# A bidirectional RWKV-7 step: the next block's keys, decays and rates issued from inside the scan

## The chip, the cores and the metric

The program runs on one core of a Trainium2 chip. Its time is device time in microseconds, from launch to end of one execution. A profile is one execution taken by the hardware profiler; its span goes from the first to the last instruction, and what lies around it (some 2 us here) counts in the time but not in the span.

The engines are TensorE (PE in the profile, with its weight loads as PEld), VectorE (DVE), ScalarE (ACT), GpSimd (POOL) and SyncE (SP, which issues most of the transfers). Each works through its own queue in order, and semaphores tie the queues together.

## The reference

One layer of a diffusion backbone for 128 context tokens and 256 latent tokens with D_MODEL = 2048. A modulated RMS norm gives h; one wide projection `h @ w_in` gives the inputs of two branches; a short gated convolution (B) and an RWKV-7 mixer (A) are projected, merged by sigmoid gates and projected once more. The part that the change touches is branch A:

```python
w_lin = w0 + einsum('btdr,drc->dbtc', tanh(wd), w2)
decay = exp(-exp(-softplus(-w_lin) - 0.5))          # = exp(-e^-0.5 * sigmoid(w_lin))
a     = sigmoid(a0 + einsum('btdr,drc->dbtc', ad, a2))
kk    = k * k_k;  kk = kk / max(|kk| per head, 1e-12)
k_dir = k * (1 + (a - 1) * k_a)
# per direction, head and token:
S = S * decay + (S @ -kk) (kk * a)^T + v k_dir^T ;  y = S @ r
```

The recurrence runs forward and backward over the tokens, for 32 heads of 64 channels. Context starts from a zero state, latent tokens from a cached one. The two directions are summed, normalised per head, a bonus term is added, and the result is gated.

## The kernel before

**Layout.** Channels lie on the 128 partitions, the 384 tokens (context, then latent) along the free dimension. Branch A goes in 16 blocks of 128 channels (two heads each). Tokens go in six chunks of 64 (NCH = 6, C = 64): two of context and four latent ones. The scan is in chunk form: within a chunk the recurrence becomes triangular matrices that are inverted, between chunks a 64 x 64 state per head is carried.

**Dense stream.** `Stream` is a generator of groups of three matmuls (`mm3`, lines 81 to 83: high part by high, low by high, high by low; 128 x 384 each). It works through the wide projections, two column tiles of 128 at a time: `rk` (r and k of a block), `gv` (gate and v), and the fills `bc`, `bx`, `bg`, `gb`, `ma`, `mb` and later `ob`, `oa`. Weights are loaded by SP into two `raw` buffers and split by `split` into a high part (a cast on ACT, line 88) and a low part (a subtraction on DVE, line 89), with three buffers of each. `ds_.go(n)` emits n groups; these cover the waits of the scans.

**A block.** For block b the main loop (lines 938 to 961) runs:

- `prep_b(b)`: products of keys, rates and decays into `bk` and `pr` (lines 667 to 674), the chunk matrices `pA` (695), masked into `A` (701), and the inversion of their 32 x 32 diagonal pieces on DVE (716, 718) by way of DRAM.
- `prep_c(b)`: transposes and the value products.
- `prep_a(b + 1)`, as soon as `gv` of block b is done: for the next block the squares of the keys, the low-rank products for decay and rate and their sigmoids (`sig`, 628), the per-head norm by a matmul (`pn`, 633 and 634), floored on DVE (`kn`, 636). Its tail is elementwise: three reciprocals (638), a product with the keys (639), and for each direction a cumulative sum over a chunk (646), two exponentials on ACT (`ep`, 648; `em`, 649, written over `sig`), the direction's key `kd` (651, 652) and the rate product (653).
- `scan(b)`: the off-diagonal corners of the inverses and then the chunk chains.
- `norm(b)`; `finish(b)` follows inside the next block.

**The scan.** First the matmuls `pH` (line 847, recorded at 843) and four copies into `x11` (849), alternately on ACT and DVE; three groups of the dense stream (H0 = 3); the first state product `po` of the latent chain (805) with its sum on DVE (806); three more groups; the bonus sum `pbn` (856, 857) with `bon` on DVE (859); the matmuls `pX` (861, recorded at 843) and four copies into the corners of `A` (863), again alternately on ACT and DVE: the first two fill the corners of the even blocks of A, the others those of the odd ones. Four groups follow (H1 = 4), and then the two chains, context and latent, take turns. A step of a chain is one of: `po` (805) followed by a sum on DVE (806); `pq` (822) with A, followed by copies on ACT (824); `pu` (829) followed by a new state on DVE (832 or 834). Two groups of the dense stream lie behind each step while both chains run, four when one is left. `ls` (810) scales the old state on ACT.

**What sets the order.** PE's order is the order in which the program emits its instructions (`manual_schedule` for PE). For all other engines and for the transfers that they issue, a planner makes the order ahead of time: it takes, among the instructions that it reckons ready, the one with the best priority, which is the place in the program; `tc.high_priority(offset=300)`, which `drive(scan(b, cur), 300)` puts around the scan's own instructions, moves those 300 places forward. The order so found is fixed in the queues, whatever the real durations are. `tc.issue_after(ins)` adds for each instruction in its scope that runs on the engine of `ins` the rule that it stands behind `ins` in that queue.

Of the kernel before, what the change touches and what calls it, by code (L numbers as in the profile page):

```python
# [20 lines left out]
NB = 16  # L21
C = 64
# [34 lines left out]
def hybrid_step(ctx, tc, cst, x_prompt, x_sample, state_f, state_b, c, c_ctx, ada_w, ada_b, norm_g,  # L57
# [3 lines left out]
    V, S, G, TE = nc.vector, nc.scalar, nc.gpsimd, nc.tensor  # L61
# [339 lines left out]
    r_, k_, v_, ga_ = {}, {}, {}, {}  # L401
# [206 lines left out]
    def prep_a(b, o):  # L608

        bs = slice(b * P, (b + 1) * P)  # L610
        r, k, v = r_[b], k_[b], v_[b]
        kk = sp.tile([P, T], F32, tag="kk", name=f"kk_{b}")
        S.mul(kk[:], k[:], pcol(KK + b))
        sq = tmp(f"sq_{b}")
        S.activation(sq[:], kk[:], AF.Square)
        sqh, sql = hl_parts(sq, sp.tile([P, T], F32R, tag="hl", name=f"sqh_{b}"), f"sq_{b}")
        sig = []
        for m in range(4):
            if m % 2 == 0:
                lraw = sp.tile([96, 2, P], F32, tag="lraw", name=f"lraw_{b}_{m}")  # L620
                nc.sync.dma_start(lraw[:], (w2, a2)[m // 2][0][:, :, bs].rearrange("d r n -> r d n"))
                lwh, lwl = split(lraw[:], [96, 2, P], "lwh", "lwl", sp, f"{b}_{m}", rows=96)
                yield 2
            pl = bank(f"pl_{b}_{m}")
            pl = flat(pl[:, 0:3, :])
            mm3(pl, lwh[:, m % 2, :], lwl[:, m % 2, :], l_hi[:, m, :], l_lo[:, m, :], True, True)
            t = tmp(f"sig_{b}_{m}")
            S.activation(t[:], pl, AF.Sigmoid, bias=pcol((W0, W0 + 16, A0, A0 + 16)[m] + b))
            sig.append(t)
            yield 2  # L630
        pn = bank(f"pn_{b}")
        pn = flat(pn[:, 0:3, :])
        TE.matmul(pn, bones_r[:], sqh[:], start=True, stop=False)
        TE.matmul(pn, bones_r[:], sql[:], start=False, stop=True)
        kn = sp.tile([P, T], F32, tag="kn", name=f"kn_{b}")
        V.tensor_scalar(kn[:], pn, 1e-24, None, ALU.max)
        for q in range(3):
            V.reciprocal(kn[:, q * P:(q + 1) * P], kn[:, q * P:(q + 1) * P])
        V.scalar_tensor_tensor(kn[:], kk[:], -1.0, kn[:], ALU.mult, ALU.mult)
        o.update(kk=kk, ep=[], em=[], kd=[], bn=[])  # L640
        for d in range(2):
            def nat(a):
                return a[:, ::-1] if d else a[:]
            sg, aa = sig[d], sig[2 + d]
            L = tmp(f"L_{b}_{d}")
            V.tensor_tensor_scan(L[:], segm, sg[:], 0.0, op0=ALU.mult, op1=ALU.add)
            ep = eps_[b % 2, d]
            S.activation(ep[:, :, 1:C + 1], c3(L[:]), AF.Exp, scale=-DECAY)
            S.activation(sg[:], L[:], AF.Exp, scale=DECAY)
            kd = tmp(f"kd_{b}_{d}")  # L650
            V.tensor_scalar(kd[:], aa[:], pcol(KA + b), omka[:, b:b + 1], ALU.mult, ALU.add)
            V.tensor_tensor(kd[:], nat(k), kd[:], ALU.mult)
            V.tensor_tensor(aa[:], nat(kn), aa[:], ALU.mult)
            o["ep"].append(ep)
            o["em"].append(sg)
            o["kd"].append(kd)
            o["bn"].append(aa)
# [127 lines left out]
    def scan(b, o):  # L785
# [72 lines left out]
        bon = sp.tile([P, T], F32, tag="bon", name=f"bon_{b}")  # L858
        V.tensor_tensor(bon[:], pbn, v_[b][:], ALU.mult)
        o["bon"] = bon  # L860
        pz = corner("pX", lambda f, h: x11[32:64, 2 * f + h, :], lambda f, h: A[32:64, 0, f, C * h + 32:C * h + C])
        for j in range(4):
            (S.copy, V.tensor_copy)[j % 2](A[0:32, 0, j // 2::2, C * (j % 2) + 32:C * (j % 2) + C], pz[j])
        yield H1

        live = [chain(0), lat]
# [54 lines left out]
        V.tensor_tensor(ya[:], ya[:], ga_[b][:], ALU.mult)  # L921
        nc.sync.dma_start(ya_d[b], ya[:])

    def drive(gen, prio=0):
        n = 0
        while True:
            with tc.high_priority(offset=prio):
                u = next(gen, None)
            if u is None:
                return n  # L930
            ds_.go(u)
            n += u

    ds_.go(PRO)
    cur = {}
    drive(prep_a(0, cur))
    prev = None
    for b in range(NB):
        if b < NB - 1:
            if b > 0:  # L940
                ds_.urgent += [(add_rk, b + 1), (add_gv, b)]
        if b == NB - 2:
            ds_.fills += [(add_gv, NB - 1)] + [(add_ob, g) for g in range(8)]
        pb_gen = prep_b(b, cur)
        ds_.go(next(pb_gen))
        if prev is not None:
            finish(b - 1, prev)
        drive(pb_gen)
        n = drive(prep_c(b, cur))
        nxt = {}  # L950
        if b < NB - 1:
            while f"gv{b}" not in ds_.done:
                ds_.go(1)
                n += 1
            n += drive(prep_a(b + 1, nxt))
        w = WINDOW + (FIRST if b == 0 else LAST if b == NB - 1 else 0)
        if n < w:
            ds_.go(w - n)
        drive(scan(b, cur), 300)
        norm(b, cur)  # L960
        prev, cur = cur, nxt
    ds_.go(12)
# [180 lines left out]
```

## Time and profile before

| | us |
|---|---|
| three runs | 2264.18, 2262.54, 2259.86 |
| their median | 2262.54 |
| profiled execution, time | 2259.46 |
| profiled execution, span | 2257.7 |
| PE busy (matmuls) | 2187.7 (97%) |
| PE busy (weight loads) | 2072.2 (92%) |
| DVE busy | 1522.4 (67%) |
| ACT busy | 1048.9 (46%) |
| POOL busy | 118.6 (5%) |

The mean granted clock of PE was 0.996. The profile gives, for each line of the kernel, engine and operation, how often it ran, its busy time, the mean length of one in ns, and the engine's idle time just ahead of it with the work that ended it. A wait is written as `engine tile line <- releaser: us in total, times, longest us`. A row of a timeline is `start, length, engine, line, operation, output <- inputs, count`, with the idle time ahead in brackets.

### The profile page before, as it was taken

The numbers are of one execution on the slowest core, as the hardware profiler recorded it, in microseconds if no ns is written. First come the engines' busy times: TensorE is split into PE (matmuls) and PEld (weight loads), VectorE is DVE, ScalarE is ACT, GpSimd is POOL, SyncE is SP. The second block draws the span as 40 slices with busy tenths as digits, with TensorE's granted clock in tenths as the row PEclk, the third lists the DMA queues.
The fourth block names the chain that finished last, engine by engine and source line by source line (L and its number), as shares of the span: only waits on it lengthen the run. The fifth ranks groups of instructions, "written<-read, shape, count | busy, mean of one in ns | idle before, by whom it ended". The sixth has DMA issues, their size and how long they took to land.

```text
span 2257.7 us, 40435 instructions
## 1 busy us (share of the span) xinstructions
PE 2187.7 (97%) x16084; PEld 2072.2 (92%) x16084; DVE 1522.4 (67%) x3096; ACT 1048.9 (46%) x1852; POOL 118.6 (5%) x115
## 2 busy tenths in 40 slices
PE   5999999999999999999999999999999999999998
PEld 3588999999999999999999999999999899889988
DVE  3249567777777778776878687777767774444444
ACT  4246445454545455454545454545455543333233
POOL 2001010101010100000010101010100000000000
PEclk9999999999999999999999999999999999999999
DMA  9963544444444444353444444444445465985633
GB/s 334 347 203 116 147 137 126 114 121 114 110 132 112 125 116 126 105 132 102 122 108 132 111 112 127 113 115 141 121 118 143 133 187 161 309 299 190 219 131 113
DMA packets 429646, 339.97 MB, mean 151 GB/s; under 512 B 84801, under 2 KB 411025, under 8 KB 428561
## 3 DMA queue, kind: packets, MB, share of 16 engines
q1 hardware_dynamic: 427968, 335.62, 50.6%
q8 instruction: 127, 2.08, 0.4%
q10 hardware_dynamic: 432, 1.57, 0.2%
q14 instruction: 63, 0.51, 0.1%
q0 software_dynamic: 1056, 0.19, 0.1%
HBM read 307.37 MB, written 29.36 MB: 149 GB/s over the span
## 4 chain that ended last, share of the span: by engine, by line
PE 90%; DMA 5%; DVE 2%; issue 2%; SPq 1%; ACT 1%; POOLq 0%; POOL 0%; DVEq 0%; ACTq 0%
PE d_rk L81 4%; PE d_gv L81 4%; PE d_gv L83 4%; PE d_gv L82 4%; PE d_rk L83 4%; PE d_rk L82 4%; DMA raw_adah<-in_ada_w_dram 3%; PE d_oa L81 2%; PE d_bx L81 2%; PE d_bg L81 2%; PE d_bc L81 2%; PE d_mb L81 2%; PE pq L822 2%; PE d_bg L83 2%; PE d_bg L82 2%; PE d_bx L83 2%
## 5 line engine op out<-in xcount | busy, mean ns | idle before, releaser
L716 DVE TENSOR_TENSOR ut<-U 48x30 f32<-48x30 f32 (+14 forms) x480 | 154.6, 322 | 16.2 <-DMA U<-ui 4.2
L81 PE MATMUL d_rk<-h_hi,whi_rk 128*128 128x384 f32 x480 | 164.3, 342 | 0.6 <-ACT lst L549 0.6
L718 DVE TENSOR_TENSOR U<-U,ut 48x30 f32<-48x30 f32 (+14 forms) x480 | 154.3, 321 | 10.8
L81 PE MATMUL d_gv<-h_hi,whi_gv 128*128 128x384 f32 x480 | 161.1, 336 | 0.0
L83 PE MATMUL d_gv<-h_hi,wlo_gv 128*128 128x384 f32 x480 | 160.8, 335 | 0.0
L82 PE MATMUL d_gv<-h_lo,whi_gv 128*128 128x384 f32 x480 | 160.7, 335 | 0.0
L83 PE MATMUL d_rk<-h_hi,wlo_rk 128*128 128x384 f32 x480 | 160.5, 334 | 0.0
L82 PE MATMUL d_rk<-h_lo,whi_rk 128*128 128x384 f32 x480 | 160.5, 334 | 0.0
L88 ACT CAST whi_gv<-raw_gv 128x1024 fp32r<-128x1024 f32 (+1 forms) x64 | 64.0, 999 | 141.1 <-PE d_rk L82 93.9
L89 DVE TENSOR_TENSOR wlo_rk<-raw_rk,whi_rk 128x1024 fp32r<-128x1024 f32 x60 | 72.9, 1218 | 44.6 <-ACT whi_rk L88 35.5
L88 ACT CAST whi_rk<-raw_rk 128x1024 fp32r<-128x1024 f32 x60 | 63.0, 1053 | 78.7 <-PE d_bx L82 16.4
L910 POOL TENSOR_TENSOR rs<-var,nhalf 128x6 f32<-128x6 f32 x16 | 21.2, 1326 | 1370.2 <-DVE var L908 1370.2
L81 PE MATMUL d_bg<-h_hi,whi_bg 128*128 128x384 f32 x256 | 92.8, 363 | 0.0
L81 PE MATMUL d_gb<-h_hi,whi_gb 128*128 128x384 f32 x256 | 92.5, 361 | 0.0
L81 PE MATMUL d_bc<-h_hi,whi_bc 128*128 128x384 f32 x256 | 92.4, 361 | 0.0
L81 PE MATMUL d_bx<-h_hi,whi_bx 128*128 128x384 f32 x256 | 92.3, 361 | 0.0
L81 PE MATMUL d_ma<-h_hi,whi_ma 128*128 128x384 f32 x256 | 92.0, 359 | 0.0
L81 PEld LDWEIGHTS d_rk<-h_hi,whi_rk 128*128 128x128 f32 x480 | 90.1, 188 | 1.8 <-ACT lst L549 0.9
L81 PEld LDWEIGHTS d_gv<-h_hi,whi_gv 128*128 128x128 f32 x480 | 90.5, 189 | 0.2
L81 PE MATMUL d_mb<-h_hi,whi_mb 128*128 128x384 f32 x256 | 90.6, 354 | 0.0
L82 PEld LDWEIGHTS d_gv<-h_lo,whi_gv 128*128 128x128 f32 x480 | 90.4, 188 | 0.0
L83 PEld LDWEIGHTS d_gv<-h_hi,wlo_gv 128*128 128x128 f32 x480 | 90.4, 188 | 0.0
(320 smaller groups left out, 6649.5 us busy)
## 6 DMA issues: line engine op xcount, KB each, us to landing
raw_adah<-in_ada_w_dram SPq DMA_DIRECT2D x64, 512.0 KB, 8.7
raw_rk<-in_w_in_dram SPq DMA_DIRECT2D x60, 512.0 KB, 5.3
raw_gv<-in_w_in_dram SPq DMA_DIRECT2D x60, 512.0 KB, 5.0
raw_ma<-in_w_in_dram SPq DMA_DIRECT2D x16, 1024.0 KB, 5.5
raw_mb<-in_w_in_dram SPq DMA_DIRECT2D x16, 1024.0 KB, 5.4
raw_bc<-in_w_in_dram SPq DMA_DIRECT2D x16, 1024.0 KB, 5.6
raw_bx<-in_w_in_dram SPq DMA_DIRECT2D x16, 1024.0 KB, 5.5
raw_bg<-in_w_in_dram SPq DMA_DIRECT2D x16, 1024.0 KB, 5.4
```

Source lines behind the costliest of these rows:

```text
L81: TE.matmul(out, wh, xh, start=start, stop=False)
L82: TE.matmul(out, wh, xl, start=False, stop=False)
L83: TE.matmul(out, wl, xh, start=False, stop=stop)
L88: S.copy(hi[0:rows], src)
L89: V.tensor_tensor(lo[0:rows], src, hi[0:rows].bitcast(F32), ALU.subtract)
L716: V.tensor_tensor(tv, U[:, 0:s, s:s + 1].broadcast_to([48, s, w]), U[:, s:s + 1, s + 1:].broadcast_to([48, s, w]), ALU.mult)
L718: V.tensor_tensor(U[:, 0:s, s + 1:], U[:, 0:s, s + 1:], tv, ALU.add)
L822: TE.matmul(pq[:, d, :], A[:, 0, f, :], sav[:, f, :], start=True, stop=True)
L910: G.tensor_tensor(rs[:], var[:], nhalf[:], ALU.pow)
```

## The change

`prep_a` is cut in two behind the floor on the norm (line 636). What stood behind it (lines 637 to 657: reciprocals, product with the keys, cumulative sums, exponentials, keys and rate products) becomes `prep_k`. For block 0 it is called right behind `prep_a`. For blocks 1 to 15 it is called from inside the scan of the block before: `drive` gets a step (3) and a function, and calls it ahead of the scan's fourth step, when the scan has emitted the four copies of line 863 and the four groups behind them. There `prep_k` is emitted at ordinary priority, with the rule that its ACT instructions stand behind the last ACT copy and its DVE instructions behind the last DVE copy. No instruction is added to or taken from the computation.

```diff
     def prep_a(b, o):
 ...
         kn = sp.tile([P, T], F32, tag="kn", name=f"kn_{b}")
         V.tensor_scalar(kn[:], pn, 1e-24, None, ALU.max)
+        o.update(kk=kk, kn=kn, sig=sig)
+
+    def prep_k(b, o):
+
+        k, kk, kn, sig = k_[b], o["kk"], o["kn"], o["sig"]
         for q in range(3):
             V.reciprocal(kn[:, q * P:(q + 1) * P], kn[:, q * P:(q + 1) * P])
         V.scalar_tensor_tensor(kn[:], kk[:], -1.0, kn[:], ALU.mult, ALU.mult)
-        o.update(kk=kk, ep=[], em=[], kd=[], bn=[])
+        o.update(ep=[], em=[], kd=[], bn=[])
         for d in range(2):
 ...
+        o["turn"] = [None, None]
         pz = corner("pX", lambda f, h: x11[32:64, 2 * f + h, :], lambda f, h: A[32:64, 0, f, C * h + 32:C * h + C])
         for j in range(4):
-            (S.copy, V.tensor_copy)[j % 2](A[0:32, 0, j // 2::2, C * (j % 2) + 32:C * (j % 2) + C], pz[j])
+            o["turn"][j % 2] = (S.copy, V.tensor_copy)[j % 2](
+                A[0:32, 0, j // 2::2, C * (j % 2) + 32:C * (j % 2) + C], pz[j]).ins
         yield H1
 ...
-    def drive(gen, prio=0):
-        n = 0
+    def drive(gen, prio=0, at=None, fn=None):
+        n = i = 0
         while True:
+            if i == at:
+                fn()
+            i += 1
             with tc.high_priority(offset=prio):
                 u = next(gen, None)
 ...
     drive(prep_a(0, cur))
+    prep_k(0, cur)
 ...
-        drive(scan(b, cur), 300)
+
+        def keys():
+
+            with tc.issue_after(cur["turn"][0]), tc.issue_after(cur["turn"][1]):
+                prep_k(b + 1, nxt)
+
+        drive(scan(b, cur), 300, 3 if b < NB - 1 else None, keys)
```

More of the change, by code (lines that the diff above doesn't have):

```diff
@@ L610, in prep_a @@
         bs = slice(b * P, (b + 1) * P)
-        r, k, v = r_[b], k_[b], v_[b]
+        k = k_[b]
         kk = sp.tile([P, T], F32, tag="kk", name=f"kk_{b}")
```

## The prediction

> **What bounds the kernel now.** I read the page's shares and chain first, then the waits of PE and of its weight loads, then the timelines of two blocks, one that waits at the corners and one that does not.
>
> ```profile
> span 2257.7 us, 40435 instructions
> PE 2187.7 (97%) x16084; PEld 2072.2 (92%) x16084; DVE 1522.4 (67%) x3096; ACT 1048.9 (46%) x1852; POOL 118.6 (5%) x115
> PE 90%; DMA 5%; DVE 2%; issue 2%; SPq 1%; ACT 1%; POOLq 0%; POOL 0%; DVEq 0%; ACTq 0%
> ```
>
> PE carries 90% of the chain that ended last. The change adds no matmul, takes none away and moves none (prep_k holds none), so PE's order stays as written and only its waits can change. Of PE's 2257.7 - 2187.7 = 70.0 us without a matmul, this window of the loop over the blocks (its length, then busy PE) holds 1707.0 - 1685.1 = 21.9:
>
> ```profile
> 203.00:1910.00 1707.00, 1685.08 (x13166) 1645.32 (x13167) 1273.66 (x2701) 849.92 (x1548) 87.63 (x61) 1.00 0.45 125
> ```
>
> There one wait stands out; first the waits of the weight loads, then those of the matmuls:
>
> ```profile
> PEld pq L822 <- issue: 19.5, 10, 2.3
> PEld pX L843 <- issue: 3.7, 11, 1.2
> ...
> PE pq L822 <- issue: 16.6, 10, 2.0
> ```
>
> The first pq of the scan waits in 10 of 16 blocks. "issue" says that the profile found no releaser, so I look for it in the timeline of one such block (the third): PE, then DVE, then ACT.
>
> ```profile
> 479.70 0.82 PE L843 MATMUL pX<-A,x 32*32 32x32 f32 x48
> 484.80 0.68 PE L822 MATMUL pq<-sav,A 128*128 128x128 f32 x4 [1.97 <-issue]
> ...
> 475.97 2.57 DVE L638 RECIPROCAL kn<-kn 128x128 f32<-128x128 f32 x3
> ...
> 481.33 0.94 DVE L646 TENSOR_TENSOR_SCAN L<-cs,sig 128x384 f32<-128x384 f32 x1
> 482.19 0.52 DVE L667 TENSOR_TENSOR bk<-sig,sig 128x384 f32<-128x384 f32 x1
> 482.64 1.21 DVE L89 TENSOR_TENSOR wlo_gb<-raw_gb,whi_gb 128x1024 fp32r<-128x1024 f32 x1
> 483.78 0.54 DVE L859 TENSOR_TENSOR bon<-pbn,v 128x384 f32<-128x384 f32 x1
> 484.35 0.35 DVE L863 COPY A<-pX 32x192 f32<-32x192 f32 x1
> ...
> 482.36 0.53 ACT L648 ACTIVATE ep<-L 128x384 f32<-128x384 f32 x1 [0.39 <-DVE L L646]
> 482.79 0.51 ACT L649 ACTIVATE sig<-L 128x384 f32<-128x384 f32 x1
> 483.20 0.39 ACT L88 CAST lwh<-lraw 96x256 fp32r<-96x256 f32 x1
> 483.62 0.31 ACT L863 COPY A<-pX 32x192 f32<-32x192 f32 x1
> ```
>
> pX has ended at 480.52. Its first corner copy (ACT) starts only at 483.62, because ACT stands in its queue at the exponentials of L648, which wait for the scan L646, and that stands on DVE behind the reciprocals. The second copy (DVE, 484.35) ends at 484.70, and pq, which for its first chunk needs the even blocks of A, that is these two copies, starts 0.10 us later. So the corner copies release PE, and what is ahead of them is the next block's prep.
>
> **What the wait costs.** Now a block (the fifth) that does not wait, PE and then DVE:
>
> ```profile
> 694.96 0.62 PE L843 MATMUL pX<-A,x 32*32 32x32 f32 x48
> 697.70 0.60 PE L822 MATMUL pq<-sav,A 128*128 128x128 f32 x4
> ...
> 700.69 0.61 PE L829 MATMUL pu<-sav,bt 128*128 128x128 f32 x4
> ...
> 703.68 0.61 PE L805 MATMUL po<-st,pr 128*128 128x128 f32 x4
> ...
> 706.66 0.60 PE L822 MATMUL pq<-sav,A 128*128 128x128 f32 x4
> ...
> 696.87 0.35 DVE L863 COPY A<-pX 32x192 f32<-32x192 f32 x1
> ...
> 702.56 0.59 DVE L832 COPY st<-pu 64x128 f32<-64x128 f32 x2
> ...
> 705.93 0.42 DVE L806 TENSOR_TENSOR sav<-po,sav 64x256 f32<-64x256 f32 x1
> ```
>
> From pX to pq it takes 2.74 us, in the waiting block 5.10: 2.36 more, where the weight loads' longest wait is 2.3. I therefore take the weight loads' sum, 19.5 us. In one block the wait fell inside pX instead: 1.2 us, the longest of that row; its other ten (2.5 us together) are hand-overs that stay. I add 1.0.
>
> The clock adds one term. These are two windows of the third block: the stretch, its length, busy time of PE, PEld, DVE, ACT and POOL with their instructions, the granted clock, the DMA share and GB/s:
>
> ```profile
> 484.00:492.00 8.00, 7.20 (x38) 7.23 (x39) 7.15 (x16) 3.10 (x8) 0.00 (x0) 0.79 0.17 32
> 492.00:520.00 28.00, 28.00 (x217) 27.64 (x216) 17.42 (x35) 12.37 (x26) 0.00 (x0) 1.00 0.39 116
> ```
>
> Right behind this one wait PE ran at 0.79 over 8 us: 8 x 0.21 = 1.7 us. [...]
>
> Gain if all of it goes: 19.5 + 1.0 + 1.7 = 22.2 us.
>
> **The change part by part.** For 15 of 16 blocks the tail of prep_a is issued behind the second pair of corner copies. Its instructions:
>
> ```profile
> L638 DVE RECIPROCAL kn<-kn 128x128 f32<-128x128 f32 x48 | 43.6, 932 | 0.5
> L639 DVE SCALAR_TENSOR_TENSOR kn<-kk,kn 128x384 f32<-128x384 f32 x16 | 8.9, 554 | 0.3
> L646 DVE TENSOR_TENSOR_SCAN L<-cs,sig 128x384 f32<-128x384 f32 x32 | 30.2, 945 | 0.0
> L651 DVE TENSOR_SCALAR kd<-sig,par,omka 128x384 f32<-128x384 f32 x32 | 14.9, 465 | 0.0
> L652 DVE TENSOR_TENSOR kd<-k,kd 128x384 f32<-128x384 f32 x32 | 17.1, 535 | 0.1
> L653 DVE TENSOR_TENSOR sig<-kn,sig 128x384 f32<-128x384 f32 x32 | 17.4, 545 | 0.1
> ...
> L648 ACT ACTIVATE ep<-L 128x384 f32<-128x384 f32 x32 | 16.8, 525 | 14.3 <-DVE L L646 14.1
> L648 ACT ACT_TABLE_LOAD x16 | 20.5, 1283 | 5.4 <-DVE L L646 5.3
> L649 ACT ACTIVATE sig<-L 128x384 f32<-128x384 f32 x32 | 16.4, 513 | 0.1
> L863 ACT COPY A<-pX 32x192 f32<-32x192 f32 x32 | 9.9, 310 | 17.4 <-DVE A L863 12.4 <-PE pX L843 4.7
> ```
>
> The last row is a copy that stays. Per block, by busy time over 16: DVE (43.6 + 8.9 + 30.2 + 14.9 + 17.1 + 17.4) / 16 = 8.3 us in 12 instructions; ACT (16.8 + 20.5 + 16.4) / 16 = 3.4 us. No DMA is issued by it, and nothing on POOL or in SP's queue moves past it.
>
> *Ahead of the copies* this goes away. DVE keeps the maximum on kn, copies, bon and the splits. With the queues clear, the four copies follow pX one after another, as each waits for the one before (12.4 us of ACT's idle time is put down to DVE's copy): about 0.35 us each (0.31 on ACT, 0.35 on DVE), and the second ends near 0.9 us after pX's end, 1.5 after its start. pq is due 2.74 after it. The margin is 1.2 us, which is one split (1.21) that may still stand in the way. I cost new waits at pq at nothing; without that margin they would be a few tenths.
>
> *Behind the copies* 8.3 us of DVE work now stand among the first steps of the two chains. In the fifth block a step's result has from po (703.68) to pq (706.66), 2.98 us; less 0.61 for the matmuls and 0.42 for the sum of L806, some 1.95 us are free. There L806 began at 705.93, that is 1.64 us after po's end at 704.29, and PE did not wait: 0.3 us were left. Before the change that late start came from a DVE queue that had been full since ahead of the corner; now it begins clear at the copies, and the full stretch begins there. The scan's own instructions stand 300 higher in priority, so among ready ones they go first, but a queue written ahead of time can be late by as much as the real durations exceed those it was planned by. No row of the changed order exists, so I bound it: at best nothing (steps stay inside 1.95 us); at worst all 8.3 us stand ahead of the first L832. Copies end 2.1 after pX, the burst at 10.4, L832 (0.6) at 11.0; po is due at 703.68 - 694.96 = 8.7 after pX: 2.3 us a block, 15 blocks, 34 us. I take 0.2 us a block, 3 us, much nearer the low end, because in the fifth block much the same DVE work, with the chains' instructions in it, made this step 1.64 late and cost nothing.
>
> *ACT*: table load and exponentials wait for L646, some 4 us behind the copies, then hold ACT for up to 3.4. The copies L824 of both chains are due before (pq at 2.74 and about 1.5 later), the next at 706.66 - 694.96 = 11.7. If that cover goes, the price is one step of up to 1.3.
>
> *Late next*: the next block's bk products (L667, L668) move from about 482 to about 495; their reader, the next pA, is at 525. DVE is busy 17.4 of the 28 us from 492 to 520, so 10.6 are free for some 7 shifted. The split L89 comes later too, with two of three weight buffers filled ahead. Both cost nothing; without that room pA would wait for the excess, up to a few us.
>
> Sum: 22.2 - 3 = 19.2. The profiled execution took 2259.46 us (span 2257.7), so 2240.3 for one like it; the median of the runs shown is 3.1 higher, at 2262.54, and gives **2243.3**.
>
> **The rivals.**
> (a) *Half taken back*: the chains' steps wait about 0.9 us a block; 22.2 - 15 x 0.9 = 9 us, 2254. For it speaks the 0.3 us left in the fifth block; against it the many later steps that start at once.
> (b) *No change*: another full queue takes the place of the prep. If DVE's splits and ACT's casts, ready at that time, are issued into the gap, two of them (1.21 + 1.05) ahead of the copies spend the margin and another microsecond; with what the chains lose the gain is 22.2 - 10 x 1.1 - 15 x 0.5 = 4, 2259 or above. Or the order does not do what it says because the copies were late for another cause; the 0.10 us between copy and pq speak against that.
> (c) *Slower*: the moved burst holds the first chain steps. The place is L832 and L806 behind the reciprocals; price 34 us at worst, 2262.5 - 22.2 + 34 = 2274; it decides once the wait passes 22.2 / 15 = 1.5 us a block, since all 15 blocks pay and only ten gain. Against it: prep_k's instructions are short ones (0.95 at most) between which the planner can put the chains'. [...]
>
> **How the numbers follow.** Forecast 0.62; (a) 0.15; (b) 0.12; (c) 0.11. A measurement of this kernel can tell about 0.2%, 4.5 us, from no change, so faster means below 2258: forecast and (a), 0.77; within 0.12; slower 0.11. The range runs from 2238 (22.2 us gained, nothing lost, and some 2 us for the runs' scatter of 2259.86 to 2264.18) up to 2257, where (a) ends: 2238 to 2257, leaving out most of (b) and (c), 0.2.
>
> **What would show it.** Right: the pq row of L822 among the waits falls from 19.5 to under 3; the second copy of L863 stands within 1.5 us of pX's start; pX to pq is 2.74 in all blocks; the reciprocals stand behind the copies; no granted clock below 1 behind a corner. Small waits of po, pq or pu by DVE L832, L834 or L806 of 0.2 us a block would fit. Wrong: such waits above 1.5 us a block (c), or corner copies still 3 us behind pX with splits or casts ahead of them (b); pA waiting for L667 would mean that the shifted work found no room.

## The result and the profile after

| | before | after |
|---|---|---|
| median of the runs of the comparison, us | 2264.05 (2259.86 to 2268.76) | 2250.85 (2248.88 to 2255.54) |
| ratio to before, 95% interval | 1 | 0.9941 [0.9925, 0.9957] |
| profiled execution, time, us | 2259.46 | 2250.97 |
| profiled execution, span, us | 2257.7 | 2249.2 |

The changed kernel is faster by 13.2 us by the medians (9.7 to 17.0 by the interval), against 19.2 forecast. 2250.85 lies in the range and 7.6 above the predicted 2243.3. Of the runs further down, prio and sig each had one execution of more than double the time (6369.04 and 5683.89 us), which the medians count and the ratios leave out.

The head of the page of the changed kernel and the chain that ended last:

```profile
span 2249.2 us, 40427 instructions
PE 2191.4 (97%) x16084; PEld 2071.0 (92%) x16084; DVE 1522.2 (68%) x3096; ACT 1060.7 (47%) x1864; POOL 115.5 (5%) x115
PE 84%; DVE 6%; DMA 6%; ACT 2%; issue 1%; SPq 1%; POOLq 0%; POOL 0%; DVEq 0%; ACTq 0%
```

PE carries 84% of the chain instead of 90%, DVE 6% instead of 2%. A kernel that had only lost its waits would show more of PE. The 12 further instructions on ACT are table loads, 45 of 1283 ns each where before has 33; in the trace of after they stand at the exponentials of L653 (22 of them) and at the sigmoids of lines 258, 434, 480 and 488 (23). The waits of PE's weight loads in the loop say where DVE and ACT came in:

```profile
PEld pu L834 <- ACT sav L829: 8.2, 11, 0.9
PEld pA L700 <- issue: 6.3, 30, 0.2
...
PEld pq L827 <- DVE sav L811: 3.8, 6, 0.8
...
PEld po L810 <- issue: 3.0, 7, 0.6
```

(Lines have moved by 5 to 7: 822 is now 827, 829 is 834, 805 is 810, 863 is 869, 646 is 651, 832 is 837, 882 is 889.) The row of 19.5 us, pq behind the corner copies, is gone. In its place are three rows that did not stand there before: pu waiting for the copies of pq on ACT, pq for the sum of po on DVE, and po, where the row names no releaser; in the eighth block po waits for the new state on DVE (L839), at 1028.95. They are steps of the chains, behind the corner.

The eighth block is one where this is seen whole. PE, then DVE, then ACT:

```profile
1008.15 0.62 PE L848 MATMUL pX<-A,x 32*32 32x32 f32 x48
1010.97 0.68 PE L827 MATMUL pq<-sav,A 128*128 128x128 f32 x4
...
1020.66 0.71 PE L827 MATMUL pq<-sav,A 128*128 128x128 f32 x4 [0.45 <-DVE sav L811]
...
1024.33 0.71 PE L834 MATMUL pu<-sav,bt 128*128 128x128 f32 x4 [0.41 <-ACT sav L829]
...
1041.86 1.62 PE L889 MATMUL py<-sav,A 128*64 128x64 f32 x48
```

```profile
1010.52 0.35 DVE L869 COPY A<-pX 32x192 f32<-32x192 f32 x1 [1.05 <-ACT A L869]
...
1011.53 2.55 DVE L643 RECIPROCAL kn<-kn 128x128 f32<-128x128 f32 x3
1014.01 0.88 DVE L651 TENSOR_TENSOR_SCAN L<-cs,sig 128x384 f32<-128x384 f32 x1
1014.82 1.19 DVE L89 TENSOR_TENSOR wlo_bg<-raw_bg,whi_bg 128x1024 fp32r<-128x1024 f32 x1
1016.04 0.59 DVE L837 COPY st<-pu 64x128 f32<-64x128 f32 x2
...
1019.21 0.95 DVE L651 TENSOR_TENSOR_SCAN L<-cs,sig 128x384 f32<-128x384 f32 x1
1020.19 0.42 DVE L811 TENSOR_TENSOR sav<-po,sav 64x256 f32<-64x256 f32 x1
```

```profile
1009.75 0.41 ACT L88 CAST lwh<-lraw 96x256 fp32r<-96x256 f32 x1 [1.57 <-DMA lraw<-in_w_dram]
1010.18 0.31 ACT L869 COPY A<-pX 32x192 f32<-32x192 f32 x1
...
1014.19 1.28 ACT L653 ACT_TABLE_LOAD   x1
1015.49 0.52 ACT L653 ACTIVATE ep<-L 128x384 f32<-128x384 f32 x1
...
1020.19 0.52 ACT L653 ACTIVATE ep<-L 128x384 f32<-128x384 f32 x1 [1.24 <-DVE L L651]
1020.74 0.53 ACT L822 COPY ytok<-po 64x128 f32<-64x128 f32 x2
1021.18 0.52 ACT L654 ACTIVATE sig<-L 128x384 f32<-128x384 f32 x1
1021.61 1.04 ACT L88 CAST whi_bg<-raw_bg 128x1024 fp32r<-128x1024 f32 x1
...
1023.11 0.62 ACT L464 ACTIVATE bu<-bc,par 128x384 f32<-128x384 f32 x1
1023.75 0.53 ACT L829 COPY sav<-pq 64x128 f32<-64x128 f32 x2
```

The corner is as forecast: both first copies are done at 1010.87, pq starts at 1010.97, 2.82 after pX, and the reciprocals stand behind the copies. The cost comes later, on two queues:

- **DVE**: reciprocals, one scan and a split stand ahead of the first state copy (L837, at 1016.04). The second scan ends only at 1020.16, and right behind it the sum L811, at 1020.19, is already late for pq.
- **ACT**: the second direction's exponentials wait 1.24 us for that scan and stand, with copies to ytok and a cast between them, and an instruction of the convolution branch (L464) behind them, ahead of the copy L829. pq had ended at 1020.66 + 0.71 = 1021.37, and its copy starts at 1023.75, 2.4 us later. pu waits for it. The exponentials themselves fill only the first 0.3 of these 2.4 us; the rest is other work that stands ahead of the copy in the queue and was held up with it.

**A measure for the rest of the text.** An undisturbed block takes 33.1 us from the start of pX to the end of its last py: in the fifth block of before, where pX starts at 694.96, py stands at

```profile
726.46 1.62 PE L882 MATMUL py<-sav,A 128*64 128x64 f32 x48
```

so 726.46 + 1.62 - 694.96 = 33.1. In the eighth block above it is 1041.86 + 1.62 - 1008.15 = 35.3, an excess of 2.2. Summed over the 16 blocks, the excess is 23.0 in before and 14.7 in after; at the corner (pX to pq beyond 2.74) it is 20.1 and 0.1. The rest of the loop takes the same in both (1090.1 and 1090.6). Of before's 23.0, 20.1 lie at the corner, 1.7 in the clock behind the third block's corner wait, and 1.2 in small waits of 0.1 to 0.2 a block. The first two are gone; the small ones have grown from 1.2 to 14.6. So 13.4 us came back in the chains, 0.9 us a block in 15 blocks.

### The profile page after: what moved, and what is told of

It reads as the page before. It is cut to its first block, busy times and chain, and to the rows that moved or that the text cites. A ratio compares the mean times of both kernels' runs of the same rounds, so it can differ in the third digit from the quotient of the medians.

```text
span 2249.2 us, 40427 instructions
## 1 busy us (share of the span) xinstructions
PE 2191.4 (97%) x16084; PEld 2071.0 (92%) x16084; DVE 1522.2 (68%) x3096; ACT 1060.7 (47%) x1864; POOL 115.5 (5%) x115
## 3 DMA queue, kind: packets, MB, share of 16 engines
q8 instruction: 127, 2.08, 0.4%
## 4 chain that ended last, share of the span: by engine, by line
PE 84%; DVE 6%; DMA 6%; ACT 2%; issue 1%; SPq 1%; POOLq 0%; POOL 0%; DVEq 0%; ACTq 0%
PE d_rk L81 4%; PE d_rk L83 4%; PE d_rk L82 4%; DMA raw_adah<-in_ada_w_dram 4%; PE d_gv L81 4%; PE d_gv L83 4%; PE d_gv L82 4%; PE d_oa L81 2%; PE pA L700 2%; PE d_oa L83 2%; PE d_oa L82 2%; PE d_mb L81 2%; PE d_bc L81 2%; PE d_gb L81 2%; PE d_bg L81 2%; PE d_mb L83 2%
```

## The experiments

Every kernel below has its profiled time, the excess as defined (summed over its 16 blocks by its own trace), its waits of the weight loads of po, pq and pu together (each from 0.1 us up, so that a sum can be some tenths above the rows shown), and the median and ratio of its runs. "Time less excess" is what the kernel would take without the waits, and the falls of the clock, inside the scans.

| kernel | profiled time | excess | time less excess | waits of po, pq, pu | median | ratio to before |
|---|---|---|---|---|---|---|
| before | 2259.46 | 23.0 | 2236.5 | 19.6 | 2264.05 | 1 |
| again | 2266.31 | 26.5 | 2239.8 | 21.1 | one run | - |
| after | 2250.97 | 14.7 | 2236.3 | 15.5 | 2250.85 | 0.9941 [0.9925, 0.9957] |
| after2 | 2251.18 | 13.0 | 2238.2 | 13.9 | 2253.41 | 0.9952 [0.9940, 0.9964] |
| prio | 2257.70 | 18.2 | 2239.5 | 15.4 | 2257.49 | 0.9974 [0.9965, 0.9984] |
| sig | 2250.12 | 11.9 | 2238.2 | 12.9 | 2252.32 | 0.9950 [0.9937, 0.9964] |
| recip | 2250.26 | 12.7 | 2237.6 | 13.6 | 2252.66 | 0.9951 [0.9938, 0.9963] |
| marks | 2254.19 | 14.4 | 2239.8 | 14.0 | 2255.10 | 0.9963 [0.9949, 0.9977] |
| both | 2247.54 | 9.4 | 2238.1 | 9.5 | 2249.37 | 0.9937 [0.9925, 0.9949] |
| late | 2244.02 | 4.0 | 2240.0 | 3.7 | 2244.57 | 0.9916 [0.9902, 0.9929] |
| split | 2240.78 | 1.1 | 2239.7 | 0.5 | 2241.42 | 0.9903 [0.9889, 0.9916] |

The fourth column stays within 2236.3 to 2240.0 while the excess goes from 26.5 to 1.1: in these kernels the time follows the excess, about 1 us for 1 us. (h1, cover and half change PE's order itself and stand further down.)

### The kernel before once more (again)

No edit; one profile of the unchanged kernel.

> The kernel before, unchanged, for a second profile. Open: the profiled executions differ by 8.5 us in span (2257.7 and 2249.2), the medians by 13.2. Theory (clock): a corner wait of about 2 us sometimes drops PE's clock for some us; the first profile has this behind one of ten waits (granted clock 0.79 over 8 us, 1.7 us lost), another execution has it behind more, and its span is longer by some 1.7 us for each: with 2264 us, two to four drops. Rival: no more than one drop, and the span is longer elsewhere (the loading prologue, the tail).

The excess is 26.5, 3.5 more than in the first profile, with the same corner part (19.9). What differs is the clock. The three longest corner waits (2.4 us from pX to pq beyond 2.74) fall in blocks 3, 7 and 11; behind all three PE runs slower here, where the first profile shows it behind the first of them alone. The windows behind those three waits in the second profile, and then behind the first two of them in the first (stretch, length, busy PE, PEld, DVE, ACT, POOL, granted clock, DMA share, GB/s):

```profile
484.00:489.00 5.00, 4.69 (x21) 4.72 (x22) 4.97 (x10) 2.40 (x6) 0.00 (x0) 0.66 0.00 0
911.00:916.00 5.00, 5.00 (x26) 5.00 (x25) 4.31 (x9) 2.09 (x5) 0.00 (x0) 0.66 0.01 2
1338.00:1343.00 5.00, 5.00 (x25) 5.00 (x24) 4.26 (x10) 1.88 (x5) 0.00 (x0) 0.66 0.08 7
```

```profile
484.00:489.00 5.00, 4.20 (x20) 4.23 (x21) 4.94 (x11) 2.40 (x6) 0.00 (x0) 0.73 0.00 0
911.00:916.00 5.00, 4.76 (x32) 4.79 (x33) 4.94 (x11) 2.41 (x6) 0.00 (x0) 1.00 0.01 2
```

Each costs 5 x 0.34 = 1.7 us. So the change removes, beside the waits, one to three of these drops, and which of them an execution has is not the same from one to the next (what decides it was not shown). That is part of why the medians differ by 13.2 us where the two profiles differ by 8.5. The time less excess also differs, by 3.3, between the two profiles of the same kernel; that lies outside the scans of the loop's blocks and isn't the change's. One such part is a fall of the clock behind a wait of pv ahead of the last block's scan: again has it (at 1819, the wait 2.5 us), the profile of after too (0.50 from 1806.45 to 1809.87, the wait 2.9 us), the first profile of before has not (the wait 2.4 us).

### Only the place in the program (prio)

`prep_k` called where the change calls it, without the rule on the queues:

```diff
-            with tc.issue_after(cur["turn"][0]), tc.issue_after(cur["turn"][1]):
-                prep_k(b + 1, nxt)
+            prep_k(b + 1, nxt)
```

> prep_k emitted at the scan's fourth step as in the change, but without the two rules that put it behind the corner copies. Theory (the rule does it): the planner takes prep_k's instructions as soon as they are ready, ahead of the copies, and the wait of the first pq is back at 15 to 20 us by the weight loads; ratio to before 0.998 to 1.002. Rival (the place in the program does it): the copies go first by priority alone, the wait stays at 0, ratio 0.994 as in the change.

14.7 of the 20.1 us stay at the corner, a little less than expected, and the ratio is a little below the 0.998 expected. In the third block the planner takes the reciprocals and the first scan into DVE's idle time ahead of the copies all the same:

```profile
476.09 2.57 DVE L643 RECIPROCAL kn<-kn 128x128 f32<-128x128 f32 x3
...
481.45 0.94 DVE L651 TENSOR_TENSOR_SCAN L<-cs,sig 128x384 f32<-128x384 f32 x1
...
484.48 0.35 DVE L869 COPY A<-pX 32x192 f32<-32x192 f32 x1
```

So it is the rule on the queues that moves the work. The later place alone gives 0.9974, about half of the change's gain.

### No table loads, and fewer reciprocals behind the corner (sig, recip)

Two candidates for what the chains wait for. In sig the exponentials of the moved part become sigmoids, so that they need no table load in these blocks; the decays then have other values, the work has the same size. In recip the three reciprocals stay in `prep_a`:

```diff
-            S.activation(ep[:, :, 1:C + 1], c3(L[:]), AF.Exp, scale=-DECAY)
-            S.activation(sg[:], L[:], AF.Exp, scale=DECAY)
+            S.activation(ep[:, :, 1:C + 1], c3(L[:]), AF.Sigmoid, scale=-DECAY)
+            S.activation(sg[:], L[:], AF.Sigmoid, scale=DECAY)
```

```diff
         V.tensor_scalar(kn[:], pn, 1e-24, None, ALU.max)
+        for q in range(3):
+            V.reciprocal(kn[:, q * P:(q + 1) * P], kn[:, q * P:(q + 1) * P])
...
     def prep_k(b, o):
...
-        for q in range(3):
-            V.reciprocal(kn[:, q * P:(q + 1) * P], kn[:, q * P:(q + 1) * P])
```

> The change, with the four exponentials of prep_k replaced by sigmoids of the same size (so decays and their inverses are other numbers): ACT then has no table to load between them and the gates' sigmoids. The changed kernel has 12 table loads more than before and waits 8.2 us at pu for ACT's copies L829. Theory (tables): those waits fall below 2 us and the time by 5 to 8 us, ratio to before 0.990 to 0.992. Rival (the burst on DVE): ACT's copies are late because the steps ahead of them are late on DVE; the waits at pu stay above 5 us and the time within 2 us of the change, ratio 0.993 to 0.995.

> The change, with the three reciprocals left in prep_a, ahead of the corner copies; the other 5.5 us of DVE work stay behind them. Theory (the burst on DVE): with a third of the burst gone the chains' waits (15 us at pu, pq and po by the weight loads) fall below 6 us, the corner wait stays away since DVE had 2 us of idle time there, ratio to before 0.989 to 0.991. Rival (ACT): the chains' waits stay above 10 us, ratio 0.993 to 0.995. Second rival: the reciprocals hold up the copies of pH and pX and the first pq waits again by more than 5 us, ratio 0.996 or more.

sig has 1 table load in the whole program where after has 45; its excess falls by 2.8 against after and by 1.1 against after2 (the same kernel in a second comparison), and its ratio is theirs. pu still waits 7.4 us for ACT. That is the rival's side: the loads are not what decides. In the eighth block of after a load took 1.28 us, and the exponential stands directly behind it (1014.19 + 1.28, then 1015.49).

recip takes 2.7 us a block (43.6 / 16) off DVE's stretch behind the corner, and the excess goes from 14.7 (13.0 in after2) to 12.7 only, against the theory that the size of the burst sets the waits (below 6 us, ratio 0.989 to 0.991). The kinds change: pu's waits fall from 8.4 to 5.7, po's rise from 3.0 to 7.9. The fourth block of recip, on PE and DVE:

```profile
591.23 0.71 PE L834 MATMUL pu<-sav,bt 128*128 128x128 f32 x4
```

```profile
588.65 0.53 DVE L644 SCALAR_TENSOR_TENSOR kn<-kk,kn 128x384 f32<-128x384 f32 x1
...
593.12 0.55 DVE L658 TENSOR_TENSOR sig<-kn,sig 128x384 f32<-128x384 f32 x1
593.68 0.59 DVE L837 COPY st<-pu 64x128 f32<-64x128 f32 x2
```

All nine remaining instructions of the moved part stand in a row ahead of the first state copy, although that copy is 300 places ahead in priority: pu had ended at 591.94, the copy starts 1.74 later. With less work there the planner put the whole of it into the gap. That it is the order in which the queue is given, and not the amount, is tested by split and late below.

### The changed kernel once more (after2), and more cover (h1, cover, half)

after2 is the changed kernel unchanged, in another comparison. The other three leave the elementwise work alone and give PE more of the dense stream to do at the place of the wait: h1 is the kernel before with eight groups behind the corner instead of four (H1), and four fewer in `prep_b` (PB0):

```diff
-    PB0, PB1, H0, H1, CH0, CH1 = 14, 6, 3, 4, 2, 4
+    PB0, PB1, H0, H1, CH0, CH1 = 10, 6, 3, 8, 2, 4
```

cover is the changed kernel with three groups instead of two behind each step (CH0), three instead of four where one chain is left (CH1), and two fewer in `prep_b`:

```diff
-    PB0, PB1, H0, H1, CH0, CH1 = 14, 6, 3, 4, 2, 4
+    PB0, PB1, H0, H1, CH0, CH1 = 12, 6, 3, 4, 3, 3
```

half is the changed kernel with three groups behind each step in the first eight blocks, and nothing taken away for them:

```diff
+        ch0 = CH0 + 1 if b < 8 else CH0
...
-                        yield CH1 - CH0
+                        yield CH1 - ch0
...
-                    yield CH0 if len(live) > 1 else CH1
+                    yield ch0 if len(live) > 1 else CH1
```

> The changed kernel, unchanged, as the mark for the runs beside it and for a second profile. Theory (clock): without the corner waits no drop of the granted clock is seen inside the blocks, and the profiled span stays within 2 us of 2249.2. Rival: drops appear at other places of the blocks too, and its span scatters as that of before did (2257.7 and 2264.5).

> The kernel before, prep not moved, with 8 instead of 4 groups between pX and the first pq and 10 instead of 14 behind the products of prep_b. Theory (cover): the corner wait (2.4 us at most, 20 in all) is shorter than the 2.1 us added, so it falls below 2 us in sum, the clock drops behind it with it; ratio to before 0.990 to 0.992. Rival (the debt on DVE): the corner wait went with DVE and ACT catching up; without it the chains' steps wait as they do in the changed kernel, by 8 to 15 us, ratio 0.994 to 0.997.

> The change, with the dense stream's groups laid out otherwise: three instead of two behind each step while both chains run (some 11 groups more a block), three instead of four behind the steps of the single chain and 12 instead of 14 behind the products of prep_b (some 10 fewer). Work and the number of blocks' phases stay. Theory (the chains' steps are late on DVE and ACT by a little more than what covers them): 0.52 us more of cover on each side of a step ends the waits at pu, pq and po (15 us by the weight loads), ratio to before 0.987 to 0.990. Rival (what is late stays late: DVE is short of time over the whole scan): the waits move to the single chain's steps and to the next block's pA, ratio 0.993 to 0.996.

> The change with three instead of two groups of the dense stream behind each two-chain step in blocks 0 to 7, and two as before in blocks 8 to 15; nothing else is cut. Theory (a step's cover is short by a few tenths): in blocks 0 to 7 the waits at pu, pq and po are gone (under 1 us in sum) and blocks 8 to 14 keep theirs (some 1 us a block); the time falls by 5 to 8 us against the change, unless the fills that were moved forward are missed at the end. Rival (the lateness grows with the cover): blocks 0 to 7 wait as long as blocks 8 to 14.

after2: 0.9952 with an excess of 13.0; what comes back is 11.8 us here, 13.4 in the first comparison. Its span is 2249.4, and no granted clock below 1 is found inside the scans, as the theory of the clock had it: the waits of po, pq and pu, 13.9 us, are enough for the whole excess.

h1: 1.0007 [0.9998, 1.0015], no gain, where both forecasts had one. Its corner wait is gone without any move of the elementwise work, and the steps behind wait instead:

```profile
PEld po L805 <- issue: 9.7, 13, 1.2
PEld pq L822 <- DVE sav L806: 6.2, 12, 0.9
```

The excess is 49.9; the four added groups are 12 matmuls at 0.173 us (the median from start to start in the dense stream of before), 2.08 us a block, which leaves 49.9 - 16 x 2.08 = 16.6, of which 1.1 at the corner. So about 15 us turn up in the chains here too, with the elementwise work where it was before: DVE comes out of the corner with a debt, and the chains with two groups behind each step have no room to pay it off. The groups taken from `prep_b` also bring PE to the corner earlier, so the debt in h1 need not be quite that of before. And h1 pays for them: the rest of the loop is 1090.1 - 1066.4 = 23.7 us shorter, where 14 x 2.08 = 29.1 us of matmuls were taken from it (the stretch behind the first block keeps its number), so 5.4 are lost, and its time is no measure of the corner alone.

cover: 1.0027 [1.0018, 1.0036], slower, which neither forecast had. With three groups behind each step no pu and no pq waits, but po of the chain that is left alone has only three groups instead of four, and waits:

```profile
PEld po L810 <- issue: 16.0, 30, 0.9
```

The one size was traded for the other, so the run does not settle what the cover is worth.

half: 1.0236 [1.0221, 1.0252]. Nothing was taken away for the added groups, and the stream runs ahead of what feeds it: through the loop the low-rank products `pl` wait for their weights, and ahead of the last block's scan (1800 to 1840) `d_ob`, the output projection used as cover, waits for its inputs.

```profile
PEld d_ob L81 <- ACT ybh L503: 16.3, 7, 4.4
PEld pl L83 <- DVE lwl L89: 12.8, 11, 2.2
```

The first eight blocks come to 41.7 us beyond 33.1, of which 8 x 4.7 are the added groups (nine a block, 0.52 each); 4.1 are left, where after has 8.1 and after2 7.0 in the same blocks. So about half of the chains' waits go with one group more: neither nearly all, as the theory had it (under 1 us), nor none, as the rival had it.

### Both scans and all exponentials first (both)

With the reciprocals in `prep_a`, the two scans stand first and then the four exponentials; the products follow:

```diff
+        Ls = []
+        for d in range(2):
+            L = tmp(f"L_{b}_{d}")
+            V.tensor_tensor_scan(L[:], segm, sig[d][:], 0.0, op0=ALU.mult, op1=ALU.add)
+            Ls.append(L)
+        for d in range(2):
+            S.activation(eps_[b % 2, d][:, :, 1:C + 1], c3(Ls[d][:]), AF.Exp, scale=-DECAY)
+            S.activation(sig[d][:], Ls[d][:], AF.Exp, scale=DECAY)
...
         for d in range(2):
...
-            L = tmp(f"L_{b}_{d}")
-            V.tensor_tensor_scan(L[:], segm, sg[:], 0.0, op0=ALU.mult, op1=ALU.add)
-            ep = eps_[b % 2, d]
-            S.activation(ep[:, :, 1:C + 1], c3(L[:]), AF.Exp, scale=-DECAY)
-            S.activation(sg[:], L[:], AF.Exp, scale=DECAY)
```

> The change with the reciprocals left in prep_a and, in prep_k, both cumulative sums first and the four exponentials one after another (33 table loads instead of 45, as without the reciprocals). Theory (each is worth its part: tables some 2.8 us of the chains' 14.7 as the run with sigmoids has it, reciprocals some 2): chains' excess 9 to 11 us, ratio to before 0.991 to 0.993. Rival (the queue is refilled with other work and as late as before): excess 12 to 15, ratio 0.994 to 0.995.

Against recip, from which it differs in the order alone, pu's waits on ACT fall from 5.7 to 2.3, and po's stay (7.9, now 7.0): most of ACT's part is taken away, DVE's is left, since the seven products still stand in a row ahead of the first state copy. The excess is 9.4 instead of 12.7, as forecast; the ratio, 0.9937 [0.9925, 0.9949], is just above the forecast and overlaps recip's.

### The products behind the first states (split)

As both, and the products of direction 0 are issued behind the context chain's first state copy, those of direction 1 behind the latent chain's first state sum, in the same way in which the change itself holds back `prep_k`:

```diff
-                            V.tensor_copy(st[ch][hs, :, hs], pu[hs, 0:2, hs])
+                            w = V.tensor_copy(st[ch][hs, :, hs], pu[hs, 0:2, hs])
...
+                        o["st", ch, i] = w.ins
...
+        def keys_d(d):
+
+            with tc.issue_after(cur["st", d, 0]):
+                prep_d(b + 1, nxt, d)
+
+        at = {3: keys, 6: lambda: keys_d(0), 7: lambda: keys_d(1)} if b < NB - 1 else {}
+        drive(scan(b, cur), 300, at)
```

> As the last kernel (reciprocals in prep_a, both cumulative sums and the exponentials behind the corner copies), and the rest of prep_k, 3.6 us of DVE work, behind later marks: the product with the keys and direction 0 behind the context chain's first state copy, direction 1 behind the latent chain's first state sum. The amount of DVE work is the same. Theory (order, not amount: the queue puts prep ahead of the chains' instructions, which then stand behind it): the first state copy starts less than 0.5 us after its matmuls where it was 1.7 late, the chains' excess falls from 9.4 to 3 to 6 us, ratio to before 0.990 to 0.992. Rival (amount: DVE is busy through and the lateness comes back at the next step): the waits move to the sums of po one step on, excess 8 to 11, ratio 0.993 to 0.995.

2241.42 (2240.16 to 2242.93), 0.9903 [0.9889, 0.9916]: faster than both kernels, and the forecast's gain in full. The excess is 1.1, of which 0.8 at the corner of one block. The fourth block, PE and then DVE:

```profile
590.94 0.61 PE L842 MATMUL pu<-sav,bt 128*128 128x128 f32 x4
```

```profile
588.37 1.78 DVE L647 TENSOR_TENSOR_SCAN L<-cs,sig 128x384 f32<-128x384 f32 x2
591.59 0.59 DVE L845 COPY st<-pu 64x128 f32<-64x128 f32 x2 [1.44 <-PE pu L842]
```

DVE now waits for the matmul (1.44 us) and the state copy starts 0.04 after it. Over the loop, the idle time ahead of this copy shows who is late; first after, then split:

```profile
L837 DVE COPY st<-pu 64x128 f32<-64x128 f32 x32 | 9.2, 288 | 0.7
```

```profile
L845 DVE COPY st<-pu 64x128 f32<-64x128 f32 x32 | 9.2, 288 | 24.9 <-PE pu L842 24.6
```

In after DVE is never idle ahead of it (0.7 us in 32): it comes from a full queue. In split it has waited 24.6 us for PE. (A full queue alone need not cost: late, below, has 0.8 us here, and its waits come to 3.7 us in all.)

### The marks without the early exponentials (marks), and the reciprocals put back (late)

Two kernels take split apart. marks is the changed kernel with split's marks, but each direction's scan, exponentials and products together behind them. late is split with the three reciprocals again behind the corner copies, after the scans.

The edit of marks against the changed kernel (the loop over the directions in `prep_k` becomes `prep_d`):

```diff
-        for d in range(2):
+
+    def prep_d(b, o, d):
+
+            k, kk, kn, sig = k_[b], o["kk"], o["kn"], o["sig"]
...
+            with tc.issue_after(cur["st", d, 0]):
+                prep_d(b + 1, nxt, d)
```

The edit of late against split (from `prep_a` into `prep_k`):

```diff
-        for q in range(3):
-            V.reciprocal(kn[:, q * P:(q + 1) * P], kn[:, q * P:(q + 1) * P])
...
             S.activation(sig[d][:], Ls[d][:], AF.Exp, scale=DECAY)
+        for q in range(3):
+            V.reciprocal(kn[:, q * P:(q + 1) * P], kn[:, q * P:(q + 1) * P])
```

> The change, with reciprocals and the product with the keys where it has them (behind the corner copies), and the two directions of prep_k behind the marks of the run before: direction 0 (sum, exponentials, keys, rates) behind the context chain's first state copy, direction 1 behind the latent chain's first state sum. This is the order alone: the DVE work behind the copies is the changed kernel's 8.3 us, and only its place among the chains' instructions differs. Theory (order): the chains' excess falls from 13 to 15 us to 2 to 5, ratio to before 0.990 to 0.992. Rival (the amount behind the copies counts too, and the split kernel gained because the reciprocals were gone from there): 7 us or more stay, ratio 0.993 or more.

> As the kernel in which the keys' products stand behind the chains' first states (both scans and then all exponentials first, products of direction 0 behind the context chain's first state, those of direction 1 behind the latent chain's first sum), with one difference: the three reciprocals, which there stayed in prep_a, are again behind the corner copies, after the scans. Theory now: what the chains wait for is decided by two places, exponentials that reach ACT early and products behind the first states; 2.8 us of reciprocals between the scans and the first state are room that VectorE has. Then the waits of pq, pu and po together stay below 5 us (0.7 in the kernel with the reciprocals in prep_a, 15.5 in the changed kernel), and the ratio to the kernel before is 0.990 to 0.992. Rival: it is the amount of VectorE's work behind the copies that counts, whatever its order; 2.8 us more a block in 15 blocks then bring po's waits back to 7 us or more, and the ratio is 0.993 or above.

marks: 0.9963 [0.9949, 0.9977], excess 14.4, as the change itself, and by these numbers the rival's side. The kind has turned: pu for ACT is 9.6 of the 14.0 us. ACT in its fourth block:

```profile
601.00 0.53 ACT L658 ACTIVATE sig<-L 128x384 f32<-128x384 f32 x1
601.54 0.53 ACT L833 COPY sav<-pq 64x128 f32<-64x128 f32 x2
```

The exponentials, held back with the scans, run up to 601.53, and the copy of pq (matmuls done at 598.68 + 0.71 = 599.39) starts 2.15 late. The theory that the order on DVE alone decides falls with this run.

late: 0.9916 [0.9902, 0.9929], excess 4.0. In its fourth block the reciprocals take 2.54 us of the room ahead of the first state copy. The copy starts at 592.95, 0.94 us behind pu's end where it was 0.04 in split, and PE does not wait there:

```profile
590.38 2.54 DVE L651 RECIPROCAL kn<-kn 128x128 f32<-128x128 f32 x3
592.95 0.59 DVE L845 COPY st<-pu 64x128 f32<-64x128 f32 x2
```

So with all of the moved work still behind the corner, order alone takes the excess from 14.7 (13.0) to 4.0; the last 2.9, between late and split, are the reciprocals in that place. That was the theory's side of this run (waits below 5 us, ratio 0.990 to 0.992); the rival, that the amount counts whatever the order, had 7 us or more of po's waits.

## Why the prediction was right or wrong

**Right: what was removed.** The wait at pq was the corner copies' and theirs was the next block's prep: the row of 19.5 us is gone, pX to pq is 2.74 in 15 blocks (to 0.05) and 2.82 in one, the reciprocals stand behind the copies, and no granted clock below 1 is found behind a corner (1.00 over 484 to 489, 911 to 916 and 1338 to 1343). prio shows that the rule on the queues does it. The margin was real and needed: in the eighth block the second copy starts 2.37 after pX, since a cast on ACT that waited for its transfer stood ahead of the first, not within 1.5 as I wrote; five of the 16 blocks are beyond 1.5.

**Wrong: the term of 0.2 us a block for the moved burst.** It measured 13.4 us in 15 blocks (11.8 in after2), 0.8 to 0.9 us a block instead of 0.2, which is the price of rival (a). I took it "much nearer the low end", since in an undisturbed block "much the same DVE work" made a step 1.64 us late at no cost. That block was read wrongly as evidence. It had 0.3 us left, and its reciprocals, its first scan and three of its seven products had run ahead of the first corner copy on DVE (696.87); one scan and four products stood behind it:

```profile
688.89 0.95 DVE L646 TENSOR_TENSOR_SCAN L<-cs,sig 128x384 f32<-128x384 f32 x1
...
694.41 0.95 DVE L638 RECIPROCAL kn<-kn 128x128 f32<-128x128 f32 x1
...
697.61 0.94 DVE L646 TENSOR_TENSOR_SCAN L<-cs,sig 128x384 f32<-128x384 f32 x1
```

In the changed kernel all of it stands there: three products, three reciprocals and a scan more, the last two 3.4 us by the rows of the eighth block. recip, both and split show what decides on DVE: whether the products stand ahead of the first state copy. h1 speaks for a debt that was there in before too, hidden behind the corner wait: take that wait away, by cover or by order, and some 13 to 15 us turn up in the chains.

**Wrong: ACT at nothing.** The largest of the three rows is pu behind ACT (8.2 us). I had the exponentials some 4 us behind the copies, in one piece. That holds for the first direction (1014.01 for its scan, 3.1 us behind the copies); the second direction's scan begins 8.3 us behind them, because DVE does steps of the chains and a split in between, and its exponentials come just when the second round of pq is to be copied, at 12 us behind pX, the very step that I had named as the next due (11.7). The price that I named if that cover is gone, up to 1.3 us for a step, held as a bound: the longest such wait is 0.9. both, with the exponentials earlier, takes pu's waits from 5.7 in recip to 2.3; marks, with them late, has 9.6. The table loads, 12 more, are not it (sig).

**Rightly put at nothing:** the next pA's waits are 6.3 us in 30 places before and after, and no row of splits came up.

**Half right: the clock.** The measured drop was rightly counted, but as one in ten; the second profile of before has three, 1.7 us each. So the gain at the corner differs from one execution to the next, and the profile that I summed had the smaller one.

**The sum.** By the profiles: 2240.3 forecast, 2250.97 measured, 10.7 too low. Forecast was an excess of 23.0 - 19.2 = 3.8, it is 14.7, so the given-back term accounts for 10.9. For the median I added 3.1 to the profile; measured is 0.1 below it, which by luck took 3.2 off the error, and 7.6 remain. 2250.85 is nearer to the 2254 of rival (a), half taken back, than to the forecast; it lies in the range because the range was drawn to take in (a), to which I gave 0.15. The slower rival (c) did not come: the planner did put the chains' instructions between the burst's, in after at least (L837 stands ahead of the second scan), and its point of 1.5 us a block was passed only in four blocks. Of (b), splits and casts in the gap, the eighth block has a little.

**Open.** Why the planner, with a priority of 300 places, leaves nine instructions ahead of the state copy in recip: its reckoned times are not in the trace. And what the cover of one group more would be worth with the stream balanced, which cover and half do not separate.

## What to carry to other kernels

A wait that a full queue causes can be paid once for several later deadlines (here 20.1 us went at the corner and 13.4 came back in the chains): before removing it, list the next readers of that queue behind it, and count what the moved work does to each, on every engine it touches, with no lead in hand. Where queues are ordered ahead of time, priority need not protect a short step of a chain from long ready work: here it did not (in recip the state copy starts 1.74 us late). A mark (work issued behind the chain's own instruction) did (in split it starts 0.04 behind its matmuls), once the work whose results feed another engine stood first and only the rest behind the mark. An undisturbed block that "has room" says nothing on how the same work fits when it begins later.

## What the runs showed of the hardware

PE's granted clock fell behind corner waits of 2.0 us (2.4 by the starts of the matmuls): 0.66 over 5 us, 1.7 us lost, behind each of the three such longest waits in again, and behind one of three in the first profile of before (0.73 over 484 to 489, then 1.00 over 911 to 916 and over 1338 to 1343) and in prio (0.70, 1.00, 1.00 over the same windows). In before the fall is to 0.50, from 486.29 to 489.71; in again the clock is 0.50 from 486 to 488. Behind the other seven corner waits of the first profile of before (1.38 to 1.95 us by the starts) there is none.

What decides between the longest ones was not shown: in the first profile of before PE stands idle for 1.97 us up to 484.80 and for 1.98 us up to 911.24, and only behind the first of the two did the clock fall.
